# Two gate projections of a hybrid decoder layer as seven block products instead of eight, set between the tiles of another projection

## The chip, the cores and the metric

The kernel runs on one core of one Trainium2 chip. The metric is the device time of one execution in microseconds; the number that counts is the median of several executions. Times from the trace come from one profiled execution and are counted from the start of its span.

## The reference, cut to what matters

One decoder layer on 256 rows of 1024 features, all in float32. The normed input `h` is multiplied by one wide matrix; its columns are cut into retention q, k, v and gate, MoBA q, k, v and gate, and two merge gates:

```python
h = rmsnorm(x, ln_w)
proj = jnp.einsum('bsd,de->bse', h, w_in)
rq, rk, rv, rg, mq, mk, mv, mg, gr, gm = jnp.split(proj, splits, axis=-1)
ret = head_groupnorm(retention(rq, rk, rv), ret_gn_w) * jax.nn.silu(rg)
ret = ret @ w_ret_o
mo = merge_heads(moba_attention(mq, mk, mv)) * jax.nn.silu(mg)
mo = mo @ w_moba_o
y = jax.nn.sigmoid(gr) * ret + jax.nn.sigmoid(gm) * mo
return rmsnorm(x + y @ w_out, final_norm_w)
```

The change concerns `rg = h @ w_in[:, 2048:3072]`, a product of 256x1024 by 1024x1024. `silu(rg)` multiplies the normed retention output.

## The kernel before, in words

**Weights.** All weight matrices are cut into 24 groups of 512 columns (`groups`, L63). Groups 0 to 9 are the retention and MoBA q, k and v; 10 and 11 are the retention gate; 12 and 13 the MoBA gate; 14 to 17 the merge gates; 18 to 23 the three output projections. A group has four chunks of 128 partitions x 2 x 512 (512 KB). `load` (L77) fetches a chunk on SP's queue into one of six `raw` buffers. `split` (L95) makes two float32r parts of it: the high part `wh` by a ScalarE copy (L108), the low part `wl` by a VectorE subtraction (L109); there are eight buffers of each, which is two groups. The normed input is kept transposed and split in the same way in `xs` (k tile, high or low, row).

**Products.** A product of full accuracy is three float32r products: high by high, high by low, low by high. "N" groups (`proj_n`, L210) give row tiles: the x tile is stationary and 512 weight columns move, three matmuls of 512 columns per k tile (L218 to L220). "T" groups (`proj_t`, L223) give feature tiles: 128 weight columns are stationary, and the x parts move, one matmul of 512 and one of 256 columns per k tile (L233, L234). Groups 10 and 11 are "N", 12 and 13 "T".

**Order.** The main loop (L567 to L585) goes through groups 2 to 21, each in two units, `u = 2g + i`. A unit first calls `stream`: two chunks of the next group are split, and two of the group after that loaded. Then come the attention pieces noted for this unit in `extra` (L527 to L543): for MoBA head h the scores (`attn_scores`), two units later the transposes of the probabilities (`attn_transpose`, whose subtraction at L291 makes the low half `pl`), and one more unit later the product with the values (`attn_pv`, L301 to L304). Heads 0 to 3 have their scores in units 13 to 16, heads 4 to 7 in units 18 to 21. Units 24 and 25 hold the silu of the retention gate (`ret_silu`, L462) and its product with the retention output (`ret_gate`, L361), units 27, 29, 31 and 33 the transposes of the result (`ret_transpose`, L367, split at L378 and L379), and unit 37 the split of the MoBA result (`moba_split`, L510, L516 and L517). Last, the unit computes two feature tiles or one row tile and takes them out of PSUM (`evac_t`, `evac_n`). The tiles of groups 10 and 11 are copied into `rgate` by ScalarE (L460); those of 12 and 13 go through a sum (L393, L395), a sigmoid (L419) and two VectorE products (L420, L421).

The program order is a priority and not the order on an engine: a scheduler goes through the list, gives each engine the first instruction that is ready in its own model and has a buffer, and fixes the order of each engine's queue by that. On the chip each engine then works its queue in order and waits by semaphores. SP's queue holds the loads in the same manner.

GpSimd, before, makes a few small subtractions for the attention (L259) and, late in the kernel, products of 256 columns (L431) and the scaling of the final norm's weights (L581).

The main loop:

```python
    for g in range(2, NG - 2):
        for i in range(2):
            u = 2 * g + i
            stream(g, i)
...
            for f, a in extra.get(u, []):
                f(*a)
            with tc.issue_after(begun) if u == 4 else nullcontext():
                unit(g, i)
```

Of the kernel before, what the change touches and what calls it, by code (L numbers as in the profile page):

```python
# [20 lines left out]
F32 = mybir.dt.float32  # L24
F32R = mybir.dt.float32r
AF = mybir.ActivationFunctionType
ALU = mybir.AluOpType
AX = mybir.AxisListType

P = 128  # L30
S = 256
D = 1024
KT = D // P
NT = S // P
# [14 lines left out]
def hybrid_kernel(ctx: ExitStack, tc, xT, x, w_in, gn_w, w_ret_o, w_moba_o, w_out, fn_w, decay, out):  # L49
# [110 lines left out]
    def norm_x(k):  # L160
        xk, h, l = xt[:, KT + k * S:KT + (k + 1) * S], xs[:, k, 0], xs[:, k, 1]
        z = wk.tile([P, S], F32, name="z", tag="z", bufs=4)
        ins = nc.vector.scalar_tensor_tensor(z, xk, lnw[:, k:k + 1], rsb, op0=ALU.mult, op1=ALU.mult)
        nc.scalar.activation(h, z, AF.Copy)  # L164
        nc.vector.tensor_sub(l, z, h.bitcast(F32))
        return ins.ins
# [56 lines left out]
    def proj_t(g, a, i):  # L223

        ps = pm.tile([P, 2, S], F32, name="ps_m", tag="m")
        cs = slice(i * P, (i + 1) * P)  # L230
        for k in range(KT):
            h, l = wh[g, k // 2][:, k % 2, cs], wl[g, k // 2][:, k % 2, cs]
            nc.tensor.matmul(ps, h, a(k), start=k == 0, stop=False)  # L233
            nc.tensor.matmul(ps[:, 0], l, a(k)[:, 0], start=False, stop=k == KT - 1)  # L234
        return ps


    qT, kT, V = {}, {}, {}
# [8 lines left out]
    def new_v(n, dt=F32):  # L247
        return ac.tile([P, GW], dt, name=n, tag="v", bufs=8)
# [275 lines left out]
    def at(u, f, *a):  # L524
        extra.setdefault(u, []).append((f, a))
# [10 lines left out]
        at(u + 3, attn_pv, h)  # L536
    for t in range(NT):
        for c in range(2):
            at(24 + t, ret_silu, t, c)
            at(24 + t, ret_gate, t, c)  # L540
    for i in range(4):
        at(27 + 2 * i, ret_transpose, i)
    at(37, moba_split)  # L543

    nc.gpsimd.dma_start(gnw, gn_w)
# [1 line left out]
    def stream(g, i):  # L547
        for c in (2 * i, 2 * i + 1):
            split(g + 1, c)
            if g + 2 < NG:  # L550
                load(g + 2, c)

    for g in range(2):
        for i in range(2):
            stream(g, i)
        if g == 0:
            x_stats()
            nc.sync.dma_start(dec, decay)
        pair = [pm.tile([P, GW], F32, name="ps_m", tag="m") for t in range(NT)] if g else ps0
        last = proj_first(g, pair)  # L560
        for t in range(NT):
            evac_n(g, t, pair[t])
        if g:
            with tc.issue_after(last.ins):
                x_stats_t()
            begun = [norm_x(k) for k in range(KT)][3]
    for g in range(2, NG - 2):  # L567
        for i in range(2):
            u = 2 * g + i
            stream(g, i)  # L570
            if u == 38:

                xr = new_v("xr", F32R)
                ir = wk.tile([P, P], F32R, name="ir", tag="p1", bufs=2)
                nc.scalar.activation(ir, ident, AF.Copy)
                nc.scalar.activation(xr[:, :S], xn[:, 1, D - S:], AF.Copy)
                nc.vector.tensor_sub(xr[:, S:], xn[:, 1, D - S:], xr[:, :S].bitcast(F32))
            if u == 40:
                fnw = ac.tile([P, D], F32, name="fnw", tag="qk", bufs=4)
                nc.sync.dma_start(fnw, fn_w.to_broadcast([P, D]))  # L580
                nc.gpsimd.tensor_scalar_mul(fnw, fnw, 2.0)  # L581
# [4 lines that stand above are left out]
# [92 lines left out]
```

## Time and profile before

| | us |
|---|---|
| median of 3 runs | 304.42 (303.76 to 304.47) |
| profiled execution, its own time | 305.6 |
| its span in the trace | 302.7 |

Rows of the profile are read like this: an instruction is named by line, engine and operation, then output <- inputs, then the shapes; `x4` is a count, and what stands in brackets behind a time line is the idle time of that engine in front of it and what ended it. PE is TensorE (PEld its weight loads), DVE VectorE, ACT ScalarE, POOL GpSimd, SP the engine whose queue issues most DMAs. Matmuls overlap, so that the time from one start to the next is what one costs.

### The profile page before, as it was taken

The page shows a single profiled execution, that of the slowest core. Times are in us where ns is not written, and L with a number is a line of the kernel's source. Part 1 is how long each engine was busy: PE and PEld are TensorE (multiplying, and loading weights), DVE is VectorE, ACT ScalarE, POOL GpSimd, SP SyncE. Part 2 cuts the span into 40 slices and gives each one's busy share as a digit, 9 for nine tenths or more (in the row PEclk, how much of TensorE's full clock was granted, in tenths as well). Part 3 has the DMA queues.
Part 4 walks back from the last instruction along what each step waited for, and adds up shares of the span by engine and source line. Part 5 has one row for each costly group of instructions (what it writes and reads, how often), then busy time and mean ns, then how long its engine had stood idle before and what let it go on. Part 6 is the DMA issues. An engine that isn't in the chain of part 4 may idle for free.

```text
span 302.7 us, 4547 instructions
## 1 busy us (share of the span) xinstructions
PE 294.2 (97%) x1628; PEld 253.1 (84%) x1628; DVE 220.7 (73%) x402; ACT 191.5 (63%) x365; POOL 28.6 (9%) x36
## 2 busy tenths in 40 slices
PE   8999989999999999999999999999999999999992
PEld 4768878999888899888888888888888888888891
DVE  3849999977699695884747899557657458899342
ACT  5778695665738676675965857757847626646231
POOL 3000000231200123200000000000000245000000
PEclk9999999999999999999999999999999999999997
DMA  6999847948174461735267185484475576440011
GB/s 184 340 397 410 309 136 222 316 154 240 51 260 126 162 209 71 246 113 197 56 221 237 44 261 146 149 279 120 157 228 174 158 252 229 143 142 1 0 69 69
DMA packets 28966, 55.08 MB, mean 182 GB/s; under 512 B 1936, under 2 KB 3984, under 8 KB 28944
## 3 DMA queue, kind: packets, MB, share of 16 engines
q1 hardware_dynamic: 28624, 54.54, 55.4%
q8 instruction: 12, 0.20, 0.3%
q10 hardware_dynamic: 288, 0.26, 0.2%
q14 instruction: 10, 0.08, 0.1%
q0 software_dynamic: 32, 0.00, 0.0%
HBM read 53.75 MB, written 1.05 MB: 181 GB/s over the span
## 4 chain that ended last, share of the span: by engine, by line
PE 89%; DMA 4%; ACT 3%; SPq 1%; DVE 1%; issue 1%; DVEq 0%; ACTq 0%
PE ps_m L233 37%; PE ps_m L234 19%; PE ps_m L218 7%; PE ps_m L220 7%; PE ps_m L219 7%; DMA raw<-in_w_in 2%; ACT wh L108 2%; DMA xt<-in_xT 2%; PE ps_m L206 1%; PE ps_m L207 1%; PE ps_m L205 1%; PE ps_t L285 1%; SPq L87 1%; ACT xs L164 1%; PE ps_s L264 1%
## 5 line engine op out<-in xcount | busy, mean ns | idle before, releaser
L233 PE MATMUL ps_m<-xs,wh 128*128 128x512 f32 x352 | 123.6, 393 | 0.8 <-ACT qT L393 0.8
L109 DVE TENSOR_TENSOR wl<-raw,wh 128x1024 fp32r<-128x1024 f32 x88 | 108.8, 1256 | 12.9 <-ACT wh L108 12.6
L234 PE MATMUL ps_m<-xs,wl 128*128 128x256 f32 x352 | 98.9, 282 | 0.0
L108 ACT ACTIVATE wh<-raw 128x1024 fp32r<-128x1024 f32 x88 | 90.5, 1053 | 7.2 <-DMA raw<-in_w_in 2.6
L233 PEld LDWEIGHTS ps_m<-xs,wh 128*128 128x128 f32 x352 | 66.0, 188 | 14.5 <-ACT qT L393 1.1
L234 PEld LDWEIGHTS ps_m<-xs,wl 128*128 128x128 f32 x352 | 66.5, 189 | 0.2
L218 PE MATMUL ps_m<-wh,xs 128*128 128x512 f32 x64 | 25.5, 398 | 0.0
L219 PE MATMUL ps_m<-wl,xs 128*128 128x512 f32 x64 | 25.3, 395 | 0.0
L220 PE MATMUL ps_m<-wh,xs 128*128 128x512 f32 x64 | 25.3, 395 | 0.0
L233 PE MATMUL ps_m<-rT,wh 128*128 128x512 f32 x64 | 22.2, 390 | 0.0
L233 PE MATMUL ps_m<-mT,wh 128*128 128x512 f32 x64 | 22.2, 390 | 0.0
L395 DVE TENSOR_TENSOR z<-ps_m,z 128x256 f32<-128x256 f32 x32 | 13.4, 419 | 11.8 <-ACT z L393 11.7
L393 ACT ACTIVATE z<-ps_m 128x256 f32<-128x256 f32 x32 | 12.1, 379 | 13.1 <-PE ps_m L234 12.9
L431 POOL TENSOR_TENSOR A<-A,gt 128x256 f32<-128x256 f32 x8 | 6.8, 855 | 120.1 <-DVE A L395 120.1
L234 PE MATMUL ps_m<-rT,wl 128*128 128x256 f32 x64 | 18.0, 282 | 0.0
L234 PE MATMUL ps_m<-mT,wl 128*128 128x256 f32 x64 | 18.0, 282 | 0.0
L220 PEld LDWEIGHTS ps_m<-wh,xs 128*128 128x128 f32 x64 | 12.0, 188 | 2.9
L206 PE MATMUL ps_m<-wl,x 128*128 128x512 f32 (+1 forms) x34 | 13.7, 404 | 0.5 <-DVE wl L109 0.5
L219 PEld LDWEIGHTS ps_m<-wl,xs 128*128 128x128 f32 x64 | 12.0, 188 | 2.5
L218 PEld LDWEIGHTS ps_m<-wh,xs 128*128 128x128 f32 x64 | 12.0, 188 | 2.5
L233 PEld LDWEIGHTS ps_m<-mT,wh 128*128 128x128 f32 x64 | 12.0, 188 | 2.5
L233 PEld LDWEIGHTS ps_m<-rT,wh 128*128 128x128 f32 x64 | 12.0, 188 | 2.5
(183 smaller groups left out, 487.2 us busy)
## 6 DMA issues: line engine op xcount, KB each, us to landing
raw<-in_w_in SPq DMA_DIRECT2D x68, 512.0 KB, 4.7
raw<-in_w_ret_o SPq DMA_DIRECT2D x8, 512.0 KB, 5.2
raw<-in_w_moba_o SPq DMA_DIRECT2D x8, 512.0 KB, 5.7
raw<-in_w_out SPq DMA_DIRECT2D x8, 512.0 KB, 5.2
raw<-in_w_in SPq DMA_DIRECT2D x7, 256.0 KB, 4.6
xn<-in_x SPq DMA_DIRECT2D x2, 512.0 KB, 8.6
xt<-in_xT SPq DMA_DIRECT2D x7, 128.0 KB, 4.7
dec<-in_decay SPq DMA_DIRECT2D x1, 768.0 KB, 9.3
```

Of the source, the lines that this page charges most:

```text
L87: nc.sync.dma_start(t[:, j, cs], src[:, k, cs])
L108: nc.scalar.activation(h, r, AF.Copy)
L109: nc.vector.tensor_sub(l, r, h.bitcast(F32))
L206: nc.tensor.matmul(ps[:, cs], xh, l, start=False, stop=False)
L218: nc.tensor.matmul(ps, a(k)[:, 0, sl], h, start=not begun and k == 0, stop=False)
L219: nc.tensor.matmul(ps, a(k)[:, 0, sl], l, start=False, stop=False)
L220: nc.tensor.matmul(ps, a(k)[:, 1, sl], h, start=False, stop=k == KT - 1)
L233: nc.tensor.matmul(ps, h, a(k), start=k == 0, stop=False)
L234: nc.tensor.matmul(ps[:, 0], l, a(k)[:, 0], start=False, stop=k == KT - 1)
L393: nc.scalar.activation(out, ps[:, 1], AF.Copy, scale=w)
L395: nc.vector.tensor_add(out, ps[:, 0], out)
L431: nc.gpsimd.tensor_mul(A[:, f], A[:, f], G[0, f])
```

## The change

The 256x1024 by 1024x1024 product is taken as 2 x 2 blocks: x has blocks of 128 rows x 512 features, the weights of 512 x 512. Eight block products become seven (the form of Strassen's scheme that Winograd gave), of sums of blocks:

- `x_sums` adds the two parts of x to float32, forms four sums of its blocks on VectorE and splits them again (ScalarE copies, VectorE subtractions).
- The weight sums are built up in two accumulators, x and y (four chunk buffers, tag `acc`). `load_block` fetches a block into one; `add_block` fetches another block into `raw` buffers and adds it in place on GpSimd, after the accumulator's last content has been split. Accumulator x holds in turn b11, then three further sums; y holds b22, then one more. Block b21 is loaded and split plainly. In all 14 chunk loads, 14 splits and 8 GpSimd additions of 128x1024, where there were 8 loads and 8 splits.
- `product` is one block product: four k tiles, three matmuls of 512 columns each.
- The products are combined in `rgate` by seven VectorE operations that read PSUM, and one ScalarE copy.
- `gate_region` writes out the order of units 20 to 27: the seven products with the eight feature tiles of groups 12 and 13 (`fill`) between them. The loop's `stream` for groups 8 and 9 now loads and splits groups 9, 12 and 13 and the first blocks.
- The silu and gate pieces go from units 24 and 25 to 28 and 29, the transposes from units 27, 29, 31 and 33 to 30, 31, 33 and 35.
- The scratch space kept for GpSimd's DMA descriptors is set to 1024.

```diff
@@ -233,6 +238,76 @@
             nc.tensor.matmul(ps, h, a(k), start=k == 0, stop=False)
             nc.tensor.matmul(ps[:, 0], l, a(k)[:, 0], start=False, stop=k == KT - 1)
         return ps
+
+
+    SP = {}
+    xtile = {}
+
+    def x_block(t, half):
+        return lambda k: tuple(xs[:, 4 * half + k, j, t * P:(t + 1) * P] for j in range(2))
+
+    def x_sums():
+
+
+        f = ac.tile([P, KT, S], F32, name="xf", tag="rgate")
+        nc.vector.tensor_add(f, xs[:, :, 0].bitcast(F32), xs[:, :, 1].bitcast(F32))
+        a11, a12, a21, a22 = (f[:, 4 * j:4 * j + 4, t * P:(t + 1) * P] for t in range(2) for j in range(2))
+        nc.vector.tensor_sub(a22, a22, a21)
+        nc.vector.tensor_sub(a21, a11, a21)
+        nc.vector.scalar_tensor_tensor(a11, a22, -1.0, a11, op0=ALU.mult, op1=ALU.subtract)
+        nc.vector.scalar_tensor_tensor(a12, a11, -1.0, a12, op0=ALU.mult, op1=ALU.subtract)
+        for n, a in ((1, a22), (2, a11), (4, a12), (3, a21)):
+            if n in (1, 2):
+                b = ac.tile([P, 2, 4, P], F32R, name="xsum", tag="qk", bufs=4)
+                h, l = b[:, 0], b[:, 1]
+            else:
+                h, l = (new_v("xsum", F32R).rearrange("p (k s) -> p k s", s=P) for j in range(2))
+            nc.scalar.activation(h, a, AF.Copy)
+            nc.vector.tensor_sub(l, a, h.bitcast(F32))
+            SP[n] = h, l
+
+    def x_sum(n):
+        return lambda k: tuple(a[:, k] for a in SP[n])
+
+    def w_block(g, half, c):
+        src = groups[g][0].rearrange("(k p) c -> p k c", p=P)
+        return src[:, 4 * half + 2 * c:4 * half + 2 * c + 2]
+
+    def load_block(n, g, half):
+        for c in range(2):
+            xtile[n, c] = wp.tile([P, 2, GW], F32, name="acc", tag="acc", bufs=4)
+            nc.sync.dma_start(xtile[n, c], w_block(g, half, c))
+
+    def add_block(n, g, half):
+        for c in range(2):
+            r = wp.tile([P, 2, GW], F32, name="raw", tag="raw", bufs=6)
+            nc.sync.dma_start(r, w_block(g, half, c))
+            nc.gpsimd.tensor_add(xtile[n, c], xtile[n, c], r)
+
+    def load_plain(n, g, half, c):
+        raw[n, c] = wp.tile([P, 2, GW], F32, name="raw", tag="raw", bufs=6)
+        nc.sync.dma_start(raw[n, c], w_block(g, half, c))
+
+    def split_block(key, n):
+        for c in range(2):
+            r = xtile[n, c] if n else raw.pop((key, c))
+            h = wp.tile([P, 2, GW], F32R, name="wh", tag="wh", bufs=8)
+            l = wp.tile([P, 2, GW], F32R, name="wl", tag="wl", bufs=8)
+            wh[key, c], wl[key, c] = h, l
+            nc.scalar.activation(h, r, AF.Copy)
+            nc.vector.tensor_sub(l, r, h.bitcast(F32))
+
+    def product(a, key):
+        ps = pm.tile([P, GW], F32, name="ps_m", tag="m")
+        for k in range(4):
+            (xh, xl), h, l = a(k), wh[key, k // 2][:, k % 2], wl[key, k // 2][:, k % 2]
+            nc.tensor.matmul(ps, xh, h, start=k == 0, stop=False)
+            nc.tensor.matmul(ps, xh, l, start=False, stop=False)
+            nc.tensor.matmul(ps, xl, h, start=False, stop=k == 3)
+        return ps
+
+    def minus_both(out, a, ps):
+        nc.vector.scalar_tensor_tensor(out, a, -1.0, ps, op0=ALU.mult, op1=ALU.subtract)
 
 
     qT, kT, V = {}, {}, {}
@@ -536,10 +611,10 @@
         at(u + 3, attn_pv, h)
     for t in range(NT):
         for c in range(2):
-            at(24 + t, ret_silu, t, c)
-            at(24 + t, ret_gate, t, c)
+            at(28 + t, ret_silu, t, c)
+            at(28 + t, ret_gate, t, c)
     for i in range(4):
-        at(27 + 2 * i, ret_transpose, i)
+        at((30, 31, 33, 35)[i], ret_transpose, i)
     at(37, moba_split)
 
     nc.gpsimd.dma_start(gnw, gn_w)
@@ -564,10 +639,94 @@
             with tc.issue_after(last.ins):
                 x_stats_t()
             begun = [norm_x(k) for k in range(KT)][3]
+    def gate_region():
+
+        nonlocal rgate
+        rgate = ac.tile([P, NT, D], F32, name="rgate", tag="rgate")
+        c11, c12, c21, c22 = (rgate[:, t, c * GW:(c + 1) * GW] for t in range(2) for c in range(2))
+
+        def fill(j):
+            evac_t(12 + j // 4, j % 4, proj_t(12 + j // 4, lambda k: xs[:, k], j % 4))
+
+        def pieces(u):
+            for f, a in extra.get(u, []):
+                f(*a)
+
+        pieces(20)
+        nc.scalar.activation(c11, product(x_block(0, 0), "b11"), AF.Copy)
+        load_block("y", 11, 1)
+        split_block("t2", "x")
+        add_block("x", 10, 1)
+        fill(0)
+        p5 = product(x_sum(1), "t1")
+        pieces(21)
+        split_block("b22", "y")
+        add_block("y", 11, 0)
+        fill(1)
+        nc.vector.tensor_add(c21, c11, product(x_sum(2), "t2"))
+        nc.vector.tensor_add(c22, c21, p5)
+        for c in range(2):
+            load_plain("b21", 10, 1, c)
+        pieces(22)
+        split_block("t3", "y")
+        fill(2)
+        fill(3)
+        for c in (0, 1):
+            split(13, c)
+            load(14, c)
+        pieces(23)
+        minus_both(c12, c22, product(x_sum(4), "b22"))
+        for c in (2, 3):
+            split(13, c)
+            load(14, c)
+        p7 = product(x_sum(3), "t3")
+        minus_both(c22, c22, p7)
+        nc.vector.tensor_add(c21, c21, p7)
+        split_block("b21", None)
+        pieces(24)
+        fill(4)
+        nc.vector.tensor_add(c11, c11, product(x_block(0, 1), "b21"))
+        split_block("t4", "x")
+        fill(5)
+        for c in (0, 1):
+            split(14, c)
+            load(15, c)
+        nc.vector.tensor_add(c21, c21, product(x_block(1, 1), "t4"))
+        fill(6)
+        for c in (2, 3):
+            split(14, c)
+            load(15, c)
+        fill(7)
+
     for g in range(2, NG - 2):
+        if g == 10:
+            gate_region()
+        if g in (10, 11, 12, 13):
+            continue
         for i in range(2):
             u = 2 * g + i
-            stream(g, i)
+            if g == 8:
+                for c in (2 * i, 2 * i + 1):
+                    split(9, c)
+                    load(12, c)
+                if i == 1:
+                    load_block("x", 10, 0)
+            elif g == 9:
+                if i == 0:
+                    x_sums()
+                    split_block("b11", "x")
+                    add_block("x", 11, 0)
+                    for c in (0, 1):
+                        split(12, c)
+                        load(13, c)
+                else:
+                    for c in (2, 3):
+                        split(12, c)
+                        load(13, c)
+                    split_block("t1", "x")
+                    add_block("x", 11, 1)
+            else:
+                stream(g, i)
             if u == 38:
 
                 xr = new_v("xr", F32R)
@@ -668,7 +827,7 @@
         "fn_w": np.ascontiguousarray(np.asarray(final_norm_w).reshape(1, D)),
         "decay": _decay_table(np),
     }
-    nc = bacc.Bacc("TRN2", target_bir_lowering=False, num_devices=1)
+    nc = bacc.Bacc("TRN2", target_bir_lowering=False, num_devices=1, dynamic_dma_scratch_size=1024)
     args = [nc.dram_tensor(f"in_{n}", a.shape, F32, kind="ExternalInput").ap() for n, a in arrays.items()]
     o = nc.dram_tensor("out_0", (S, D), F32, kind="ExternalOutput").ap()
     with tile.TileContext(nc) as tc:
```

## Rows read from the trace of the kernel before

**Rows 1.** The page's first part: busy time, share of the span, instructions.

```profile
PE 294.2 (97%) x1628; PEld 253.1 (84%) x1628; DVE 220.7 (73%) x402; ACT 191.5 (63%) x365; POOL 28.6 (9%) x36
```

**Rows 2.** The page's fourth part: the chain that ended last, by engine.

```profile
PE 89%; DMA 4%; ACT 3%; SPq 1%; DVE 1%; issue 1%; DVEq 0%; ACTq 0%
```

**Rows 3.** Timeline of TensorE around units 18 to 28: start, duration, instruction.

```profile
121.61 0.40 PE L218 MATMUL ps_m<-wh,xs 128*128 128x512 f32 x1
...
126.98 0.40 PE L220 MATMUL ps_m<-wh,xs 128*128 128x512 f32 x1
127.21 0.28 PE L301 MATMUL ps_o<-ph,vh 128*128 128x256 f32 x1
...
133.97 0.49 PE L285 MATMUL ps_t<-ident,tS 128*128 128x128 f32 x3
...
185.87 0.39 PE L233 MATMUL ps_m<-xs,wh 128*128 128x512 f32 x1
```

**Rows 4.** Busy time from 112 to 184 us: PE, PEld, DVE, ACT, POOL, clock, DMA share, GB/s.

```profile
112.00:184.00 72.00, 72.00 (x393) 62.03 (x393) 51.84 (x93) 50.65 (x102) 4.61 (x4) 1.00 0.49 161
```

**Rows 5.** VectorE's groups from 112 to 184 us: count, busy us, mean ns.

```profile
L109 DVE TENSOR_TENSOR wl<-raw,wh 128x1024 fp32r<-128x1024 f32 x21 | 25.6, 1241 | 2.5 <-ACT wh L108 2.4
...
L466 DVE TENSOR_TENSOR rgate<-rgate,sg 128x512 f32<-128x512 f32 x4 | 2.7, 688 | 4.2 <-ACT sg L465 4.1
...
L420 DVE TENSOR_TENSOR z<-z,sg 128x256 f32<-128x256 f32 x6 | 2.5, 419 | 1.0 <-ACT sg L419 1.0
...
L517 DVE TENSOR_TENSOR mT<-oT,mT 128x256 fp32r<-128x256 f32 x4 | 1.7, 417 | 0.5 <-ACT mT L516 0.5
...
L379 DVE SCALAR_TENSOR_TENSOR rT<-ps_t,gnw,rT 128x256 fp32r<-128x256 f32 x2 | 0.9, 474 | 0.0
```

**Rows 6.** ScalarE's groups from 112 to 184 us.

```profile
L108 ACT ACTIVATE wh<-raw 128x1024 fp32r<-128x1024 f32 x22 | 22.6, 1055 | 0.8 <-PE ps_m L233 0.6 <-PE ps_m L220 0.3
...
L460 ACT ACTIVATE rgate<-ps_m 128x512 f32<-128x512 f32 x4 | 2.4, 592 | 6.6 <-PE ps_m L220 6.5
```

**Rows 7.** Timelines of GpSimd (first four) and VectorE (last three), whole span.

```profile
69.61 0.46 POOL L259 TENSOR_TENSOR early<-qT,early 128x128 fp32r<-128x128 f32 x1 [2.17 <-ACT early L258]
73.71 0.74 POOL L259 TENSOR_TENSOR mk0s<-kT,mk0s 128x256 fp32r<-128x256 f32 x1 [3.65 <-ACT mk0s L258]
...
80.62 1.47 POOL L259 TENSOR_TENSOR mk0s<-kT,mk0s 128x256 fp32r<-128x256 f32 x1 [4.35 <-ACT mk0s L258]
...
253.83 3.49 POOL L581 TENSOR_SCALAR fnw<-fnw 128x1024 f32<-128x1024 f32 x1 [3.03 <-DMA fnw<-in_fn_w]
...
80.28 2.91 DVE L109 TENSOR_TENSOR wl<-raw,wh 128x1024 fp32r<-128x1024 f32 x2 [0.82 <-ACT wh L108]
...
239.71 2.36 DVE L109 TENSOR_TENSOR wl<-raw,wh 128x1024 fp32r<-128x1024 f32 x2 [0.83 <-ACT wh L108]
...
253.46 3.19 DVE L109 TENSOR_TENSOR wl<-raw,wh 128x1024 fp32r<-128x1024 f32 x2
```

**Rows 8.** Timeline of VectorE: the split of group 14's last chunk.

```profile
177.18 1.21 DVE L109 TENSOR_TENSOR wl<-raw,wh 128x1024 fp32r<-128x1024 f32 x1
```

**Rows 9.** Busy time from 112 to 120 us, columns as above, and VectorE's timeline.

```profile
112.00:120.00 8.00, 8.00 (x50) 7.18 (x50) 3.84 (x9) 5.08 (x14) 1.91 (x3) 1.00 0.37 132
...
122.84 1.21 DVE L109 TENSOR_TENSOR wl<-raw,wh 128x1024 fp32r<-128x1024 f32 x1
123.98 0.41 DVE L291 TENSOR_TENSOR pl<-ps_t,ph 128x256 fp32r<-128x256 f32 x1
```

**Rows 10.** DMA issues by line; SP's waits from 112 to 184 us (total, times, longest).

```profile
raw<-in_w_in SPq DMA_DIRECT2D x68, 512.0 KB, 4.7
...
SPq L89 <- DVE wl L109: 41.1, 13, 10.4
```

**Rows 11.** Busy time behind the stretch, columns as above.

```profile
184.00:195.00 11.00, 11.00 (x67) 9.79 (x66) 7.90 (x15) 7.25 (x15) 0.00 (x0) 1.00 0.62 191
195.00:207.00 12.00, 12.00 (x73) 10.69 (x72) 7.66 (x11) 8.17 (x15) 0.00 (x0) 1.00 0.55 177
```

## The prediction

> **What bounds the kernel now.** I read the busy table first: TensorE is busy 97% of a span of 302.7 us, VectorE 73%, ScalarE 63%, GpSimd 9% [rows 1]. The chain that ended last runs through TensorE for 89% of the span, so outside the start and the tail time is saved by fewer matmuls and lost by making TensorE wait [rows 2]. Then TensorE's order of time around the change: 23 matmuls of 512 columns start between 121.61 and 126.98 us, which is 0.2335 us each; unit 19 (the second half of group 9) begins at 127.21 and unit 20 (group 10) at 133.97 [rows 3]. No TensorE gap stands there. Last the stretch in which the new work falls: from 112 to 184 us TensorE is never idle, VectorE works 51.8 of 72 us, ScalarE 50.7, GpSimd 4.6, at a granted clock of 1.00 [rows 4]. The cover available to the new work is therefore 20.2 us of VectorE and 21 us of ScalarE.
>
> **Removed from TensorE.** Two groups on two row tiles are 2 x 2 x 8 x 3 = 96 matmuls of 512 columns; seven block products are 7 x 4 x 3 = 84. Twelve matmuls at 0.2335 us are 2.80 us, all on the path. The gate's eight feature tiles are the same matmuls, only placed between the products.
>
> **VectorE.** In this stretch a split subtraction of 128x1024 takes 1.24 us and a 128x512 operation on SBUF 0.69 [rows 5]. Sums of x: one addition of 2048 columns (1.24 plus two steps of 0.55, the difference of those rows: 2.35), four combinations and four low parts at 0.69, in all 7.9 us. Weight splits: 14 in place of 8, 6 x 1.24 = 7.4. Combining the products: seven operations at 0.69, 4.8. Out of the stretch go the four silu products (2.7), the four gate products of the same size (as much again, 5.4 together) and two transposed halves (0.9), which are moved behind it. Net 20.1 - 6.3 = 13.8 us. The stretch itself shrinks to 69.2 us, so 20.2 - 2.8 - 13.8 = 3.6 us of idle time are left, and 1.7 us more from the four MoBA halves that were done there early [rows 5]: 5.3 us.
>
> **ScalarE.** Six more splits at 1.055, four high parts and one copy at the 0.592 of a 128x512 copy, less four such copies and four sigmoids of that size [rows 6]: 6.3 + 3.0 - 2.4 - 2.4 = 4.5 us, to 55 of 69.2. Costed at nothing; were VectorE not behind it, it would have room.
>
> **GpSimd.** Eight additions of 128x1024. Its undisturbed additions took 0.46 us at 128 columns and 0.74 at 256 [rows 7], so 0.28 per 128 more: 2.42 at 1024, an estimate from these two; the one row of that width, with one input, took 3.49. Together 19 to 28 us, room enough in 69. But the two engines disturb each other. Two split subtractions that last 2.36 us undisturbed took 2.91 with a 256-column addition beside them, and that addition 1.47 in place of 0.74 [rows 7]. VectorE lost 0.55 us; in proportion, 2.2 at 1024 columns. The one-input row of 1024 columns cost the pair beside it 3.19 - 2.36 = 0.83. The loss falls on operations with two inputs in SBUF: splits 25.6 + 7.4, sums of x 7.9, the MoBA gate's two products of 2.5 each and the MoBA halves 1.7 [rows 5], 47.6 of 69.2 us, 69%. Eight additions then take 8 x 2.2 x 0.69 = 12.1 us of VectorE, between 6.6 (0.83 each) and 17.6 (all collide). I take 12.1, since the two-input rows are the same kind of operation.
>
> The Trainium skill, "GPSIMD Engine Reference", section 4.1, says to put elementwise work on VectorE and not on GpSimd, about twice as slow there. By it the eight additions would cost VectorE 8 x 1.24 = 9.9 us, less than the 12.1 that the collisions take, and the sums on GpSimd would bring nothing; no row of this case has an addition of this width on both engines.
>
> **Set against the margin.** The split of group 14's last chunk ended at 177.18 + 1.21 = 178.4, and TensorE came to that chunk at 185.87 [rows 3, 8]: splits run 7.5 us ahead. Over the stretch 12.1 us are met by 5.3 of idle time and 7.5 of margin, so the sum as a whole stalls nothing; with every addition colliding it stalls 17.6 - 12.8 = 4.8 us.
>
> **Where it is tight first: head 3.** Unit 19 begins with head 3's value product, which waits for the low half of its transposed probabilities; before, that subtraction ended at 124.39, 2.8 us ahead of 127.21 [rows 3, 9]. What is queued ahead of it now: what is left of the 7.9 us, and GpSimd's first two additions behind the first block's splits. The sums of x need only xs and a buffer that is free after unit 16, and VectorE worked 3.8 of the 8 us from 112 to 120, 4.2 idle [rows 9]; that order follows readiness and not the text is shown by the split at 122.84, which belongs to unit 19's lines and went ahead of unit 18's subtraction at 123.98. So 3.7 us of the sums are left. Bounds of the wait: nothing, if they go behind the subtraction and one addition collides (2.2 against 2.8); 3.7 + 4.4 - 2.8 = 5.3 if all goes ahead. I take one collision and half of the rest, 2.2 + 1.9 - 2.8 = **1.3 us**, nearest to the row that has one addition between two splits. Everything behind head 3 on TensorE waits with it.
>
> **DMA and SP.** Fourteen block loads in place of eight, six of 512 KB more. The stretch moved 161 GB/s x 72 us = 11.6 MB, about 22 loads, at a share of 0.49 [rows 4]; with 28 it is 0.65, while a load lands in 4.7 us [rows 10]. Bandwidth costs nothing. The order does more: SP waited for VectorE's splits 41.1 us in this stretch to get raw buffers back [rows 10], and group 13's four chunks are now loaded in units 18 and 19 but split only behind the fourth feature tile, holding four of six buffers. The sums pass through the other two: the second use of accumulator x must be split (from 133.97: 1.06 + 1.24, 136.3), added to (2.42 + 1.2 of waiting, 139.9), its buffer refilled (4.7) and added (148.2), refilled and added again (156.5), split (158.8), and GpSimd's queue puts the other half before it (2.4): 161.2. TensorE wants that half of the fifth product at 133.97 + 8 x 2.80 + four attention pieces of about 1 us + 1.4 = 161.8. Costed at nothing, with 0.6 us to spare.
>
> **Behind the stretch.** From 184 to 195 us VectorE worked 7.9 of 11 us, to 207 another 7.7 of 12 [rows 11]. The moved 5.4 us fit before 207 only with a lag of up to 2.4 us inside the margin; nothing, at most 1.5. PSUM: one of four buffers stays held over two products, three are left; nothing while VectorE is less than a product (2.8 us) late.
>
> **Sum.** -2.80 + 1.3 = -1.5 us. The profiled execution took 305.6 us by its own time (2.9 above its span); it becomes 304.1, and the median of 304.42, 1.2 below it, becomes **302.9**. A difference under 0.3%, 0.9 us, can't be told from none here.
>
> **Rivals.**
> Full cover: all sums of x find idle time, no wait at head 3, 301.6. For it, 4.2 us of gaps and 13 us of reserve over the stretch; against it, the 2.8 us at head 3. Chance 0.16.
>
> The chain of sums through two raw buffers (0.6 us to spare) is late by what VectorE is behind: with a lag of 3 us the fifth product waits 2.4 us, in all -0.4, 304.0: no difference to be measured. For it SP's waits; against it that a wait at head 3 pushes the want back too. Chance 0.24.
>
> Slower: VectorE becomes the bound from unit 18 on, at the port. Place: head 3's subtraction and the splits behind it. Price 5.3 us, in all +2.5, 306.9. It decides once the wait exceeds 2.8 + 0.9 = 3.7 us, that is, if both first additions collide and more than 2.1 us of the sums stand ahead. For it, the idle rest of 3.6 us in 69; against it, the gaps before 120. Chance 0.29; a part of it, with the whole stretch colliding too (4.8 more), lies above 309.
>
> The Trainium skill, "SBUF — State Buffer", section "Who interferes with whom", goes further: a VectorE instruction with two SBUF inputs and a reading GpSimd instruction exclude each other for the whole instruction, and the later one blocks fully. By that rule an addition costs 2.42 and not 2.2, 19.4 us with all colliding. The trace agrees for short additions (0.55 of 0.74 us lost); the 3.49 us row, which cost 0.83, does not.
>
> **How the numbers follow.** Forecast 302.9, chance 0.31. Faster by over 0.3%: 0.31 + 0.16 = 0.47; within: 0.24; slower: 0.29. The range runs from full cover less the runs' scatter, 301.4, to just above the slower rival's price, 307.2; about one in ten lies above, less than one in ten below.
>
> **What would show it.** Right: 84 product matmuls, VectorE above 90% busy from 112 to 181, additions near 2.4 us, subtractions beside them near 3.4, a TensorE gap of about a microsecond in front of head 3's product and none elsewhere. Wrong: gaps in front of the products themselves (the chain of sums, or PSUM), a gap above 3 us at unit 19 (the port), or subtractions that last 1.24 beside an addition (no collision: full cover).

## The result, and the profile after

The changed kernel takes **315.09 us** in the median (four executions, 313.34 to 317.31) against 304.42: a ratio of 1.036 [1.028, 1.044], 10.7 us slower. The prediction said 302.9, with 307.2 as the upper end of its range. One execution of run 10 below, of 313.98 us, was in a slower state of the chip and is left out of the figures given for that run.

The profiled execution is the fastest of the four (313.34 us, span 311.6); the one of before was 1.2 us above its median. So the traces differ by less than the medians: 8.9 us of span. The page of the changed kernel, busy times and the chain that ended last:

```profile
PE 293.7 (94%) x1616; PEld 252.0 (81%) x1616; DVE 249.0 (80%) x424; ACT 197.2 (63%) x372; POOL 48.6 (16%) x44
...
PE 66%; DVE 22%; DMA 4%; issue 2%; ACT 2%; POOL 1%; SPq 1%; DVEq 0%; ACTq 0%; POOLq 0%
...
L285 POOL TENSOR_TENSOR acc<-acc,raw 128x1024 f32<-128x1024 f32 x8 | 20.5, 2573 | 19.9 <-DMA raw<-in_w_in 14.4
...
L298 DVE TENSOR_TENSOR wl<-acc,wh 128x1024 fp32r<-128x1024 f32 x12 | 19.9, 1669 | 2.5 <-ACT wh L297 2.5
```

TensorE has the twelve matmuls less (1616 for 1628, [rows 1]), but the chain now runs through VectorE for 22% of the span where it was 1% [rows 2]. The new splits last 1669 ns in the mean where a split of this size took 1241 [rows 5].

TensorE's waits over the whole span, the first two rows (total, times, longest):

```profile
PE ps_o L377 <- DVE pl L366: 7.0, 3, 4.7
PE ps_m L305 <- DVE wl L298: 1.4, 1, 1.4
```

TensorE's timeline of the changed kernel; a bracket is the idle time in front of an instruction and what ended it:

```profile
126.56 0.28 PE L376 MATMUL ps_o<-ph,vh 128*128 128x256 f32 x1
131.58 0.58 PE L377 MATMUL ps_o<-pl,vh 128*128 128x256 f32 x1 [4.74 <-DVE pl L366]
...
133.67 0.63 PE L223 MATMUL ps_m<-wh,xs 128*128 128x512 f32 x1
134.09 0.63 PE L224 MATMUL ps_m<-wl,xs 128*128 128x512 f32 x1
...
157.03 0.39 PE L377 MATMUL ps_o<-pl,vh 128*128 128x256 f32 x1 [0.67 <-DVE pl L366]
...
165.84 0.39 PE L377 MATMUL ps_o<-pl,vh 128*128 128x256 f32 x1 [1.58 <-DVE pl L366]
...
177.90 0.50 PE L305 MATMUL ps_m<-wl,xs 128*128 128x512 f32 x1 [1.37 <-DVE wl L298]
```

Head 3's product waits 4.74 us for the subtraction of L366 (`pl`, before L291), heads 5 and 6 wait for theirs, and the product with block b21 for its split. Two more gaps of 0.3 to 0.4 us stand between. Counted from start to start less the usual length, the six gaps are 9.7 us. Behind the long gap a 512-column matmul takes 0.42 us (133.67 to 134.09) and not 0.2335 [rows 3]: the granted clock fell. Busy time by stretches, columns as in [rows 4] (the clock is the last but two):

```profile
112.00:181.00 69.00, 60.24 (x316) 50.62 (x315) 63.79 (x88) 46.39 (x93) 26.19 (x12) 0.98 0.48 141
...
125.00:130.00 5.00, 1.84 (x9) 1.24 (x7) 5.00 (x4) 0.66 (x2) 2.81 (x2) 1.00 0.37 104
130.00:135.00 5.00, 3.42 (x13) 3.19 (x14) 4.29 (x12) 1.37 (x6) 0.00 (x0) 0.66 0.95 306
135.00:140.00 5.00, 5.00 (x25) 4.01 (x24) 3.69 (x8) 3.94 (x7) 0.00 (x0) 1.00 0.16 32
```

From 112 to 181 us VectorE is busy 63.79 of 69 us. From 130 to 135 the granted clock is 0.66: the records of matmuls are at the lower of the two levels, 1.2 GHz, for part of it. The balance from head 2's value product to the first transposed retention product: 109.0 us before, 118.1 after; 9.1 = -2.8 for the twelve matmuls, +9.7 of gaps, and the remaining 2.2 mostly the lower clock.

What held VectorE stands in its timeline:

```profile
111.90 2.27 DVE L253 TENSOR_TENSOR xf<-xs 128x2048 f32<-128x2048 f32 x1
...
121.59 0.41 DVE L470 TENSOR_TENSOR kT<-ps_m,kT 128x256 f32<-128x256 f32 x1
121.93 2.56 DVE L266 TENSOR_TENSOR xsum<-xf,xsum 128x512 fp32r<-128x512 f32 x1
124.42 1.75 DVE L298 TENSOR_TENSOR wl<-acc,wh 128x1024 fp32r<-128x1024 f32 x1
126.09 0.68 DVE L266 TENSOR_TENSOR xsum<-xf,xsum 128x512 fp32r<-128x512 f32 x1
126.70 4.49 DVE L114 TENSOR_TENSOR wl<-raw,wh 128x1024 fp32r<-128x1024 f32 x2
131.11 0.41 DVE L366 TENSOR_TENSOR pl<-ps_t,ph 128x256 fp32r<-128x256 f32 x1
...
145.98 2.32 DVE L298 TENSOR_TENSOR wl<-acc,wh 128x1024 fp32r<-128x1024 f32 x1 [2.53 <-ACT wh L297]
...
153.10 1.95 DVE L495 TENSOR_TENSOR z<-z,sg 128x256 f32<-128x256 f32 x1 [0.49 <-ACT sg L494]
...
157.35 2.83 DVE L298 TENSOR_TENSOR wl<-acc,wh 128x1024 fp32r<-128x1024 f32 x1
```

and in that of GpSimd, six of the eight additions (`x2` is a pair):

```profile
121.08 2.86 POOL L285 TENSOR_TENSOR acc<-acc,raw 128x1024 f32<-128x1024 f32 x1
...
126.25 2.72 POOL L285 TENSOR_TENSOR acc<-acc,raw 128x1024 f32<-128x1024 f32 x1 [1.16 <-DVE wl L298]
141.98 5.23 POOL L285 TENSOR_TENSOR acc<-acc,raw 128x1024 f32<-128x1024 f32 x2 [13.01 <-DMA raw<-in_w_in]
...
152.36 2.40 POOL L285 TENSOR_TENSOR acc<-acc,raw 128x1024 f32<-128x1024 f32 x1 [1.16 <-DVE wl L298]
156.72 2.38 POOL L285 TENSOR_TENSOR acc<-acc,raw 128x1024 f32<-128x1024 f32 x1 [1.96 <-DVE wl L298]
```

The four rows in front of `pl` (121.93 to 126.70) last 9.5 us; undisturbed they take 0.69 + 1.21 + 0.69 + 2.35 = 4.9. Of the other 4.5 us, 4.0 lie under the two additions that start at 121.08 and 126.25, and 0.5 (the split of 124.42) beside a small attention subtraction that GpSimd already made before the change. These 4.5 us are nearly the length of the wait at head 3. How the blocking works is plain further on. The small product `z` starts at 153.10 and usually lasts 0.42 us; it ends at 155.05, 0.3 us after the addition that began at 152.36 ended (154.76). The split of 157.35 ends 1.08 us after the addition of 156.72 does. A VectorE operation with two inputs in SBUF that comes while an addition runs stands until it is over. One with an input in PSUM does not: the sum of 121.59 takes its usual 0.41 us under the first addition. The Trainium skill, "SBUF — State Buffer", section "Who interferes with whom", says of such a pair with two SBUF inputs: whoever comes first has the shared ports for its whole instruction, and the other blocks fully. The trace agrees, 1.95 us in place of 0.42.

The additions also hold VectorE up in a second way. At 145.98 it has stood idle for 2.53 us, because the next split in its queue needs the high part of a weight sum. ScalarE makes that part as soon as the addition is done:

```profile
144.88 1.06 ACT L297 ACTIVATE wh<-acc 128x1024 fp32r<-128x1024 f32 x1 [2.90 <-POOL acc L285]
```

and GpSimd could start that addition only at 141.98, when its block had landed. Behind this idle time come the blocked operations up to 162.9. The chain that ended last goes through both, from that block's load to the product of head 6, so that both have a part in the later waits.

### The profile page after: what moved, and what is told of

The parts are those of the page before. It is cut to its first block, busy times and chain, and to the rows that moved or that the text cites. A ratio compares the mean times of both kernels' runs of the same rounds, so it can differ in the third digit from the quotient of the medians.

```text
span 311.6 us, 4576 instructions
## 1 busy us (share of the span) xinstructions
PE 293.7 (94%) x1616; PEld 252.0 (81%) x1616; DVE 249.0 (80%) x424; ACT 197.2 (63%) x372; POOL 48.6 (16%) x44
## 4 chain that ended last, share of the span: by engine, by line
PE 66%; DVE 22%; DMA 4%; issue 2%; ACT 2%; POOL 1%; SPq 1%; DVEq 0%; ACTq 0%; POOLq 0%
PE ps_m L238 27%; PE ps_m L239 14%; DVE wl L114 6%; DVE wl L298 5%; DMA raw<-in_w_in 4%; PE ps_m L223 4%; PE ps_m L224 4%; PE ps_m L225 4%; PE ps_m L211 2%; PE ps_m L210 2%; PE ps_m L212 2%; ACT wh L113 1%; DVE z L495 1%; POOL acc L285 1%; DVE xs L170 1%
## 5 line engine op out<-in xcount | busy, mean ns | idle before, releaser
L114 DVE TENSOR_TENSOR wl<-raw,wh 128x1024 fp32r<-128x1024 f32 x80 | 100.1, 1269 | 10.5 <-ACT wh L113 10.1
L113 ACT ACTIVATE wh<-raw 128x1024 fp32r<-128x1024 f32 x80 | 82.4, 1054 | 8.3 <-DMA raw<-in_w_in 2.6
L285 POOL TENSOR_TENSOR acc<-acc,raw 128x1024 f32<-128x1024 f32 x8 | 20.5, 2573 | 19.9 <-DMA raw<-in_w_in 14.4
L298 DVE TENSOR_TENSOR wl<-acc,wh 128x1024 fp32r<-128x1024 f32 x12 | 19.9, 1669 | 2.5 <-ACT wh L297 2.5
L468 ACT ACTIVATE z<-ps_m 128x256 f32<-128x256 f32 x32 | 12.1, 379 | 13.0 <-PE ps_m L239 12.9
L470 DVE TENSOR_TENSOR z<-ps_m,z 128x256 f32<-128x256 f32 x32 | 13.4, 417 | 6.9 <-ACT z L468 6.8
L297 ACT ACTIVATE wh<-acc 128x1024 fp32r<-128x1024 f32 x12 | 12.6, 1060 | 3.7 <-POOL acc L285 2.9
L349 ACT ACTIVATE tS<-tS,st 128x128 f32<-128x128 f32 (+1 forms) x16 | 7.1, 447 | 11.0 <-DVE st L347 10.7
L223 PE MATMUL ps_m<-wh,yT 128*128 128x512 f32 (+1 forms) x40 | 14.0, 350 | 0.0
L225 PE MATMUL ps_m<-wh,yT 128*128 128x512 f32 (+1 forms) x40 | 14.0, 350 | 0.0
L224 PE MATMUL ps_m<-wl,yT 128*128 128x512 f32 (+1 forms) x40 | 14.0, 350 | 0.0
```

Source lines behind the costliest of these rows:

```text
L113: nc.scalar.activation(h, r, AF.Copy)
L114: nc.vector.tensor_sub(l, r, h.bitcast(F32))
L223: nc.tensor.matmul(ps, a(k)[:, 0, sl], h, start=not begun and k == 0, stop=False)
L224: nc.tensor.matmul(ps, a(k)[:, 0, sl], l, start=False, stop=False)
L225: nc.tensor.matmul(ps, a(k)[:, 1, sl], h, start=False, stop=k == KT - 1)
L285: nc.gpsimd.tensor_add(xtile[n, c], xtile[n, c], r)
```

## The experiments

Diffs are against the changed kernel unless said otherwise. Ratios are to the kernel before, whose median was 304.1 to 304.4 us in these sessions. A gap is TensorE's, from start to start less the usual length.

**1. No additions.** This and the next three ran together.

```diff
-            nc.gpsimd.tensor_add(xtile[n, c], xtile[n, c], r)
```

> The eight GpSimd additions of weight blocks are left out; loads, splits and products stay. Collision theory: beside these additions VectorE's two-input operations lasted 12 us longer in all, 4 of it ahead of head 3's subtraction; without them that subtraction ends before 128 (131.5 in the changed kernel), the gap in front of head 3's value product shrinks from 4.9 to 1 us or less, later gaps go too, and the time falls by 6 to 9 us, to 306 to 309. Rival, the work itself: VectorE has too much to do ahead of head 3 in any case, the gap stays above 3 us and the time at 312 or more.

This kernel leaves out what the result needs; only its time is of use. 303.31 us, 0.997 [0.996, 0.999], faster than the collision theory's 306 to 309. There is one gap in the region, 0.88 us at head 3 (TensorE's timeline):

```profile
129.12 0.39 PE L376 MATMUL ps_o<-pl,vh 128*128 128x256 f32 x1 [0.72 <-DVE pl L365]
```

The eight additions carry the whole loss, 11.8 us; everything else of the change together gives 0.9 us of the 2.8.

**2. Attention pieces first.** In units 18 and 19 the pieces stand ahead of the sums of x and the splits.

```diff
             elif g == 9:
+                for f, a in extra.pop(u, []):
+                    f(*a)
```

> The attention pieces of units 18 and 19 stand ahead of the sums of x and the splits in the program, nothing else is changed. Order theory: head 3's subtraction goes ahead of the second addition and two splits, the gap at head 3 falls from 4.9 to 1 us or less with the lower clock behind it, and the time falls by 4 to 7 us, to 308 to 311. Rival, capacity: VectorE is busy 97% from 150 to 200 us whatever the order, the lost time comes back at heads 5 and 6 and at the later products, and the time stays within 2 us of the changed kernel, at 313 or more.

311.31 us, 1.025 [1.022, 1.027]: 3.8 us better than the changed kernel, between the two theories. TensorE's timeline, the value products of heads 3 and 5 (that of head 4, at 142.32, does not wait either):

```profile
126.29 0.28 PE L377 MATMUL ps_o<-pl,vh 128*128 128x256 f32 x1
...
149.88 0.50 PE L305 MATMUL ps_m<-wl,xsum 128*128 128x512 f32 x1 [1.62 <-DVE wl L298]
...
156.58 0.58 PE L377 MATMUL ps_o<-pl,vh 128*128 128x256 f32 x1 [4.98 <-DVE pl L366]
```

Head 3 no longer waits at all, and two units later a product waits 1.62 us and a head 4.98. Order at head 3 gives back a part; the rest of the lag shows elsewhere, here also in front of a product of a weight sum.

**3. Additions on VectorE.**

```diff
-            nc.gpsimd.tensor_add(xtile[n, c], xtile[n, c], r)
+            nc.vector.tensor_add(xtile[n, c], xtile[n, c], r)
```

> The eight additions are made on VectorE instead of GpSimd. Collision theory: they cost VectorE 8 x 1.24 = 9.9 us and free it of the 12 us of collisions; the time falls by 0 to 3 us, to 312 to 315. Rival, that GpSimd's additions run mostly beside VectorE's work: the time rises by 4 us or more.

304.07 us, 1.000 [0.998, 1.001], where the expectation had 312 to 315. An addition takes 1.2 us there (a pair 2.35), 2.4 on GpSimd, so that VectorE has 9.4 us of its own work in place of 12 us of blocking. VectorE's longest idle time between 112 and 182 us is now 0.73 us, for a load. Together this is worth 11.0 us of time. TensorE at head 3:

```profile
127.88 0.28 PE L376 MATMUL ps_o<-ph,vh 128*128 128x256 f32 x1
...
131.14 0.39 PE L377 MATMUL ps_o<-pl,vh 128*128 128x256 f32 x1 [1.24 <-DVE pl L366]
```

Between the two halves of head 3's product ten other matmuls now run, where they followed each other directly in the changed kernel. How much of the gain is this order is the question of run 13.

**4. No sums of x.** `x_sums()` is left out and the four products read a plain block of x.

```diff
-        p5 = product(x_sum(1), "t1")
+        p5 = product(x_block(0, 0), "t1")
```

> The sums of x are left out (7.9 us of VectorE and 2.5 of ScalarE ahead of head 3); the four products that use them take a plain block of x. GpSimd's additions stay. If the sums of x make head 3 late: its subtraction ends about 4 us earlier, the gap there falls to about 1 us, the time falls by 4 to 6 us, to 309 to 311. If the collisions do: the gap stays at 3 us or more and the time falls by 2 us or less.

312.63 us, 1.027 [1.024, 1.030]. This kernel, too, leaves out what the result needs. With 7.9 us of VectorE work gone, head 3's gap falls from 4.90 to 1.87 us, but that of head 5 grows from 0.84 to 2.29; head 6 has 0.64 (1.75 in the changed kernel), and b21 keeps its 1.52. The time falls by 2.5 us, between the two signs: the sums of x make up most of the wait at head 3 and little of the loss. TensorE at b21, and the busy times there:

```profile
175.69 0.69 PE L305 MATMUL ps_m<-wl,xs 128*128 128x512 f32 x1 [1.36 <-DVE wl L298]
...
175.00:180.00 5.00, 4.31 (x12) 3.39 (x13) 5.00 (x7) 1.72 (x3) 0.00 (x0) 0.66 0.89 304
```

The clock is at the lower level behind this short gap, where it was 1.00 from 175 to 180 us in the changed kernel, with a gap of the same size at 177.90.

**5. Value products a unit later**, from head 3 on. Runs 5 to 8 ran together.

```diff
-        at(u + 3, attn_pv, h)
+        at(u + (4 if h >= 3 else 3), attn_pv, h)
...
+        pieces(25)
```

> As the changed kernel, with GpSimd's additions, but the value product of heads 3 to 7 one unit later in the program, so that nothing on TensorE's queue waits for the low half of the probabilities for another 5 to 7 us. Theory A, the unplanned lateness: VectorE's lag of some 5 us, which the order of TensorE's queue does not allow for, is met by the longer distance; the gaps at heads 3, 5 and 6 (7.5 us and the lower clock behind) go, some at the block products stay; 305 to 308. Theory B, capacity: the lag is more than the stretch can hold, the gaps move to the block products, 311 or more.

314.77 us, 1.035 [1.033, 1.037], as theory B had it. The gaps in front of the value products are gone; in their place TensorE waits 0.86 us at 135.53 for a scaling, 3.27 us at 155.44, where that subtraction now holds up the next head's transposes, and 2.85 at 163.17, for `z` to free a PSUM buffer. Distance in one queue is not the remedy. VectorE's timeline there:

```profile
158.19 4.59 DVE L353 TENSOR_SCALAR tS<-tS,st 128x128 f32<-128x128 f32 x2
```

and GpSimd's:

```profile
157.08 5.54 POOL L285 TENSOR_TENSOR acc<-acc,raw 128x1024 f32<-128x1024 f32 x2 [2.87 <-ACT mT L591]
```

Two scalings with a single tensor input in SBUF, 0.55 us together elsewhere, stand until the pair of additions ends (162.62), the first under the first addition and the second under the other.

**6. The same, with the additions on VectorE** (diffs 3 and 5 together).

> The additions on VectorE and the value products one unit later. By theory A the 1.9 us of gaps that the additions on VectorE alone left (heads 3 and 4) go: 302 to 303.2, faster than before. If VectorE's capacity decides: no better than 304.

304.56 us, 1.002 [1.000, 1.004]: no better than run 3, which was the sign for VectorE's capacity.

**7. Additions in the kernel before.** The kernel before, with eight additions that nothing uses and the changed kernel's scratch size:

```diff
+            if g in (10, 11, 12, 13) and c < 2:
+                nc.gpsimd.tensor_add(spare, spare, r)
```

> The kernel before, with eight useless GpSimd additions of 128x1024 that read the raw chunks of groups 10 to 13 (two chunks of each). They collide with VectorE as the changed kernel's do, where VectorE has 20 us of idle time and the split weights 7 us of margin. If a collision costs only where VectorE is full or TensorE's queue is tight: at most 2 us, 304 to 306.5. If eight additions on GpSimd cost 11 us wherever they stand: 312 or more.

304.91 us, 1.002 [1.000, 1.003]. Busy time from 112 to 184 us, to be read beside [rows 4]:

```profile
112.00:184.00 72.00, 72.00 (x394) 62.04 (x393) 62.34 (x97) 51.04 (x104) 20.65 (x10) 1.00 0.52 165
```

VectorE is busy 10.5 us longer in this stretch, 9.7 of its 20.2 idle us remain, and TensorE never waits. Eight additions of the size that costs 11 us in the changed kernel cost 0.6 us here (0.1 to 1.0). Two things differ: VectorE has idle time for the blocking, and nothing waits for the sums.

**8 and 9. Softmax scaling on ScalarE**, in run 8 on top of run 6, in run 9 on top of run 3.

```diff
-            nc.vector.tensor_scalar_mul(s[:, sg], s[:, sg], st[:, 4 + j:5 + j])
+            nc.scalar.activation(s[:, sg], s[:, sg], AF.Copy, scale=st[:, 4 + j:5 + j])
```

> As the kernel with the additions on VectorE and later value products, and the softmax's scaling (0.55 to 0.7 us a head on VectorE) on ScalarE. If VectorE is still what limits the gain: 0.3 to 1 us better than without it, 301.8 to 302.8. If not: the same within 0.4 us.

> The additions on VectorE and the softmax's scaling on ScalarE, the value products where the change has them. If VectorE's load still costs the version with additions on VectorE some of its 2.8 us: 302.5 to 303.6, faster than before beyond its interval. If its gaps were only at head 3, whose wait is on VectorE's order and not its load: 303.6 to 304.4.

303.81 us, 0.999 [0.997, 1.001], and 303.84, 0.9985 [0.9972, 0.9998]. Run 9 is the only version that leaves nothing out and whose interval is clear of 1, and that just so: 0.15% faster than the kernel before. It lies where its second sign put it, with a gap left at head 3 alone.

**10 and 11. Which additions.** In run 10 the first two are on VectorE and six on GpSimd; in run 11 it is the other way round. Run 12 ran with them.

```diff
+            (nc.vector if (n, g, half) == ("x", 11, 0) else nc.gpsimd).tensor_add(xtile[n, c], xtile[n, c], r)
```

> Only the first two of the eight additions, those ahead of head 3, are made on VectorE; six stay on GpSimd. The order of TensorE's queue then differs from the changed kernel's at head 3 alone. If head 3 is the main loss (4.9 us of gap and the lower clock behind it): 307 to 309.5. If every addition costs its share, a quarter of 11 us goes: 312 to 313. If the lag only moves to the next additions: 314 or more.

> The reverse: the first two additions on GpSimd, the other six on VectorE. If head 3 is the main loss: 309 to 312, with a gap of about 5 us there and none of half a microsecond behind it. If every addition costs its share: 306 to 307.5.

310.16 us, 1.019 [1.016, 1.022], and 309.52, 1.016 [1.013, 1.020]. Against run 3 the six on GpSimd cost 6.1 us, the two 5.4; together 11.5, near the 11.0 of all eight. Run 10 fell between its signs, run 11 gave the one for head 3 as the main loss. In run 11 TensorE has one gap only in this region (its timeline):

```profile
127.61 0.28 PE L376 MATMUL ps_o<-ph,vh 128*128 128x256 f32 x1
132.64 0.58 PE L377 MATMUL ps_o<-pl,vh 128*128 128x256 f32 x1 [4.75 <-DVE pl L366]
```

and behind it the clock falls (busy time by stretches):

```profile
130.00:135.00 5.00, 2.36 (x10) 2.37 (x11) 4.29 (x8) 1.25 (x5) 0.03 (x1) 0.59 0.75 236
135.00:140.00 5.00, 5.00 (x17) 3.92 (x17) 2.97 (x9) 2.93 (x6) 0.00 (x0) 0.72 0.21 78
```

The gap is 3.5 us longer than run 3's 1.41; the other 1.9 of the 5.4 us go with the clock of 0.59 and 0.72, which in run 3 was 1.00 there. In run 10 the gaps are many and short (1.41 at head 3, 1.60, 1.53, 1.09 and smaller ones), and the clock stays at 1.00.

**12. Additions in quarters**, four of 256 columns for each.

```diff
+            for k in range(2):
+                for cs in (slice(0, S), slice(S, GW)):
+                    nc.gpsimd.tensor_add(xtile[n, c][:, k, cs], xtile[n, c][:, k, cs], r[:, k, cs])
```

> Each GpSimd addition is cut into four of 256 columns, 0.74 us each instead of 2.4, so that VectorE can come in between. If what hurts is how long one addition holds VectorE's operation back: the time falls by 3 us or more, to 312 or less. If what hurts is the total taken from VectorE (32 x 0.55 = 17.6 us if all collide, as for the long ones) and the later end of the additions: 314 to 318.

311.40 us, 1.025 [1.020, 1.030]. VectorE is busy 4.6 us less over the span (244.4 for 249.0), and head 3's gap is 2.72. 3.7 of the 11 us come back, as the first sign had it; the last 24 quarters still stand back to back on GpSimd for 21.8 us.

**13. TensorE's order pinned at head 3.** Run 3's kernel, with head 5's scores and the rest of unit 19 issued only behind head 3's value product.

```diff
+                with tc.issue_after(pv[3].ins) if u == 19 and f is attn_scores else nullcontext():
+                    f(*a)
-            with tc.issue_after(begun) if u == 4 else nullcontext():
+            with tc.issue_after(begun) if u == 4 else tc.issue_after(pv[3].ins) if u == 19 else nullcontext():
```

> All additions on VectorE, as in the run that had them there, but TensorE's order at head 3 pinned: the scores of head 5 and the rest of unit 19 are issued only behind head 3's value product, so that TensorE has no other matmuls to bring forward. Theory A (the additions on VectorE cost little because the order written ahead of time brings other matmuls in front of the late product): head 3's subtraction ended about 10.2 us behind head 2's value product in that run, against 12.0 with the additions on GpSimd; without the 11 matmuls brought forward the gap at head 3 grows from 1.4 to about 3 or 4 us, and the time from 304.07 to 305.7 or more. Theory B (only the time taken from VectorE counts, the order does not): the gap stays near 1.4 us and the time within 0.9 us of 304.07.

307.17 us, 1.009 [1.007, 1.011], 3.1 us above run 3. TensorE's timeline:

```profile
126.44 0.28 PE L376 MATMUL ps_o<-ph,vh 128*128 128x256 f32 x1
129.70 0.58 PE L377 MATMUL ps_o<-pl,vh 128*128 128x256 f32 x1 [2.99 <-DVE pl L366]
...
133.07 0.63 PE L223 MATMUL ps_m<-wh,xs 128*128 128x512 f32 x1
133.49 0.63 PE L224 MATMUL ps_m<-wl,xs 128*128 128x512 f32 x1
```

VectorE's, the subtraction that it waited for:

```profile
129.23 0.41 DVE L366 TENSOR_TENSOR pl<-ps_t,ph 128x256 fp32r<-128x256 f32 x1
```

and the busy times and the clock behind the gap:

```profile
130.00:135.00 5.00, 5.00 (x17) 4.32 (x17) 3.00 (x10) 1.75 (x6) 0.00 (x0) 0.50 0.68 239
```

VectorE is as late as in run 3: `pl` starts 9.5 us after head 2's value product in both (129.23 against 119.71; there 130.68 against 121.15). Only TensorE's order differs, and the gap grows from 1.41 to 3.14 us. Nine matmuls behind it at the lower level (0.43 us each) add 1.7. So of the 3.5 us by which run 3's gap is shorter than the changed kernel's 4.90, 1.7 come from the order, and 1.8 from VectorE, whose subtraction started 11.3 us behind head 2's value product there. Theory A holds at this place: work on VectorE is cheap where the order of TensorE's queue, fixed ahead of time, has other matmuls in front of what comes late.

**14. Run 9 with the attention pieces of units 18 and 19 first** (the edit of run 2).

> All additions on VectorE, the softmax scaling on ScalarE, and the attention pieces of units 18 and 19 written ahead of the sums of x and of the splits. Theory A (a lag on VectorE only moves to the next short wait): the gap of 1.56 us at head 3 goes, one of about the same size comes at a later head, 303.8 within 0.5. Theory B (the gap at head 3 is a matter of order alone, VectorE has the time): 1.2 to 1.6 us are gained, 302.2 to 302.6, and the change's seven products are then worth most of their 2.8 us.

303.95 us, 0.999 [0.997, 1.002]. Head 3's wait is gone and `z` is waited for instead, for 0.90 us at 155.95, as theory A had it. In the profiled execution the stretch from head 2's value product is 1.1 us shorter than run 9's (107.4 for 108.5), but its start is 1.5 us longer and the median no better; with twelve executions between 302.77 and 306.89 the gain isn't shown.

## Why the prediction was wrong

The prediction's own sign for the port, a gap above 3 us at unit 19, is what came.

**TensorE, -2.80 us: right.** 1616 matmuls for 1628; nothing of it is lost on TensorE itself.

**VectorE's new work: right, and still short.** The addition of 2048 columns took 2.27 us (2.35 expected), the others 0.69. Without additions (run 1) only 0.88 us is waited for at head 3.

**GpSimd's additions: right.** 2.38 to 2.40 us undisturbed, 2.42 expected. The Trainium skill, "GPSIMD Engine Reference", section 4.1, puts elementwise work on VectorE, as twice as fast; the runs agree (1.2 us against 2.4, and run 3 is 11.0 us faster than the changed kernel).

**The collisions: right in sum.** From 110 to 200 us VectorE's operations last 13.4 us longer than the same shapes do undisturbed; 1.4 of it stands beside the attention's old GpSimd subtractions, 12.0 beside the eight additions, 12.1 expected. That the two agree so closely is in part luck: seven of the eight additions collided, with losses of 1.1 to 2.2 us, where the sum had 5.5 of them at 2.2. That the loss falls on operations with two inputs in SBUF alone was too narrow (run 5's scalings).

**"The sum as a whole stalls nothing": this step failed.** It set 12.1 us against 5.3 us of idle time and 7.5 us by which splits run ahead of TensorE. That margin belongs to weight splits. The attention's subtractions, the transposes' inputs and the operations that free PSUM run only a few microseconds ahead (2.8 at head 3, [rows 9]), and they stand in the same VectorE queue behind the delayed splits. So the lag comes out at heads 3, 5 and 6 while no weight split is waited for before 175.6 us; then the splits' margin is gone too (0.2 us at group 13, 1.4 at b21). Runs 2, 4, 5 and 10 show the same lag in front of whichever short wait comes next, and run 7 shows it vanish where VectorE has 20 us to spare and nothing needs the sums.

**Head 3's wait, 1.3 us: mis-sized, 4.74.** Both first additions collided and all of the remaining sums, and a pair of splits, went ahead of the subtraction: what came was close to the bound of 5.3, and the choice of the middle between the bounds was wrong. The rival "slower", given a chance of 0.29, named this place and mechanism, put its decision at 3.7 us of waiting, and priced it at 5.3 us; run 11 against run 3 gives 5.4, though 1.9 of it are the lower clock and the gap alone is 3.5 longer. Its second part, "the whole stretch colliding too", was put at 4.8 us; the last six additions cost 6.1, though not all collided (12.0 us lost, not 17.6).

**The lower clock** was no term of the sum. At head 3 it is worth 1.7 to 1.9 us (runs 13, 11).

**The chain of sums, DMA, "behind the stretch", PSUM.** No TensorE wait for a sum or a load appears except b21's 1.4 us, whose block is plainly loaded and split: VectorE's lag again. So the rival of the late chain did not come as it was priced, in front of the fifth product. But the chain was not free: a block that landed at 141.9 and the addition behind it left VectorE idle for 2.53 us at 145.98, which is part of the lag behind it. In run 2 it has 2.44 us of the same at 143.58, and there a product of a weight sum, the third, does wait for its split, 1.62 us. The working set the chain only against TensorE and not against VectorE's queue.

**Full cover** needed 301.6. Even without additions (run 1) the change gives 303.31, so 1.9 us of the 2.8 are missing. In its profile the stretch from head 2's value product to the first transposed retention product takes 107.2 us, 1.8 less than before, which is the 2.8 less the gap of 0.88. The other 0.9 us stand ahead of the stretch, which starts at 121.39 where it started at 120.49; with one profile for each run the reason stays open.

What stays open: how the cost of the last six additions divides between blocking and the late sums for which VectorE stood idle, since a run without GpSimd's additions takes away both. And that the planned order leaves the collisions out is argued from runs 3 and 13, at head 3 alone; no run gave the planner the blocked durations.

## What to carry to other kernels

A GpSimd addition with two SBUF inputs is not free work beside VectorE: count most of its length as VectorE time (12.0 of 20.5 us here), and where VectorE is nearly full put it on VectorE, where it takes half as long. Set a chain of loads and sums against every queue that waits for it, not against TensorE alone. Compare a lag with the shortest distance of anything queued on that engine, not with the longest. Where the bounds of a wait are far apart and the ends are decided by which of two operations goes first, price the bad end fully, and add what the clock does behind a long gap.

## What the runs showed of the hardware

- An addition of 128x1024 on GpSimd held up a VectorE scaling with one tensor input in SBUF (a pair of additions: two scalings in 4.59 us for 0.55), as it did operations with two, but not a sum with one input in PSUM (0.41 us under an addition); the one-input GpSimd row of 3.49 us [rows 7] had cost a pair of splits only 0.83.
- After a TensorE gap of 3.1 us the granted clock was 0.50 for the next five (run 13), after 4.9 us 0.59 and 0.72 (run 11); after gaps of 1.4 to 1.6 us it stayed at 1.00 in runs 3 and 10, but with one of 1.52 us in run 4, ending at 175.69, it was 0.66 from 175 to 180 us. The length of the gap alone does not decide it.
